# First mixer of a two-block transformer kernel: q and k turned by halves of the tokens, other distances between attention steps, the last v projection moved, one-operation rotation

## The chip, the cores and the metric

The kernel runs on one core of a Trainium2 chip. The metric is the device time of one execution in microseconds (us). Of the kernel before, three runs took 3729.02, 3718.52 and 3720.03 us, a median of 3720.03 us. TensorE (PE) multiplies, PEld is its weight load, VectorE (DVE) and ScalarE (ACT) work element by element, GpSimd (POOL) does small side work, and SyncE (SP) issues the DMAs.

## The reference, cut to what matters

The whole computation is two transformer blocks of two layers each over 512 tokens of width 1024, all in fp32. Only the first layer's mixer is touched, a dilated window attention with 3 groups of 16 heads of 64:

```python
qkv = (h @ w_in).reshape(bsz, seq, 3, 3, 16, 64)
for g, (window, dilation) in enumerate(((128, 1), (512, 4), (2048, 16))):
    q = rope(rms_norm(qkv[:, :, g, 0], q_gain[g]), positions)
    k = rope(rms_norm(qkv[:, :, g, 1], k_gain[g]), positions)
    o, lse = dilated_window_attention(q, k, qkv[:, :, g, 2], window, dilation)
    outs.append(o); lses.append(lse)
alpha = jax.nn.softmax(jnp.stack(lses, axis=0), axis=0)
out = jnp.sum(alpha[..., None] * jnp.stack(outs, axis=0), axis=0)
return out.reshape(bsz, seq, 1024) @ w_out
```

`rope` turns the halves of a head: `[x1*cos - x2*sin, x2*cos + x1*sin]`.

## The kernel before, in words

Every fp32 operand is split into a high and a low fp32r part (`split`: ACT copies the high part, DVE subtracts for the low one), and a product is three matmuls: high by high, low by high, high by low. All matmuls carry line L225. The weights of a step come by DMA (`wraw`), four steps ahead, and are split into `wh` and `wl`.

The mixer (`layer_a_`, L579) works in four quarters `qd` of four heads. In each quarter the groups g = 0, 1, 2 follow each other:

- `wide` (L883) projects q and k together, 512 columns by 128 tokens, for two halves of the tokens; each half gives two PSUM banks `mm`. Per (quarter, group) that is 96 matmuls of 512 columns. `a_heads` (L545) takes each bank into `qs`, makes the norm and the rotation, and leaves `qr`, 128 tokens by 512 (four buffers, so one group). The rotation is four DVE operations on `qs`: times cosine (L561), the two crossed halves times sine (L563, twice), their sum (L565); L567 is the norm.
- `a_turn` (L650) transposes `qr` on TensorE, four 128x128 blocks into the one `sm` bank, and splits the bank into `qkH` and `qkL`; four such steps for q and k of two pairs of heads.
- v comes from `tokmajor` for g = 0, and for g = 1 and 2 together from a second `wide` behind the q, k of g = 1.
- `a_chain` (L666) is the attention of one group. For g = 0, `a_scores` and `a_near`; for the others `a_scores_far` and `a_far`: scores into `sc` banks, a masked minimum on DVE (L714, L735), exp on ACT (L716, L737) into `pm`, transposes of `pm` into the one `pt` bank, a split into `ptH`, `ptL`, and the product with v into the one `o` bank. `a_stats` turns the softmax sums; after g = 2, `a_merge` weighs the three groups: `sw` is turned into the `sm` bank and split into `swH`, `swL`, small matmuls (12 rows in) spread the weights over `sm` and `sc` banks, and DVE multiplies them into `og` and adds up (L857, L860, L861).
- `proj_out` multiplies a quarter's result with `a_w_out`. It stands behind g = 1 of quarter 1 (for quarter 0), and three times at the end: quarter 2, quarter 1 (`late`), quarter 3.

What sets the order: `a_turn`, `a_chain` and others are generators ("chains"). While `wide` and `proj_out` issue matmuls, `mul` adds their length to a clock `now`, and `tick` (L242) lets a chain go on once the distance it yielded (in ns of matmul time) has passed. `until` (L250) is a drain: it advances the chains at once, with no projection between their steps, until a condition holds. Before the next group's `a_heads` can write `qr`, the old turn must be done (`until(old.done)`); before a v tile is taken, older attention must be done. A scheduler then moves instructions locally where it finds an operand late. The projection's matmuls between attention steps are called filler below.

Of the kernel before, what the change touches and what calls it, by code (L numbers as in the profile page):

```python
# [198 lines left out]
class Net:  # L199
# [345 lines left out]
    def a_heads(self, ps, t, C, Sn):  # L545

        nc = self.nc
        p = self.ap
        qs = p.tile([P, S], F32, tag="qs", name=self.nm("qs"), bufs=1)
        nc.scalar.copy(qs, ps)  # L550
        t2 = p.tile([P, S], F32, tag="r2", name=self.nm("r2"), bufs=1)
        nc.scalar.activation(t2, qs, AF.Square)
        ss = self.tile("ss", [P, 8], bufs=3)
        nc.vector.tensor_reduce(out=ss, in_=t2.rearrange("p (h d) -> p h d", d=64), axis=AX.X, op=ALU.add)
        rs = self.tile("rs", [P, 8], bufs=3)
        nc.gpsimd.tensor_scalar(out=rs, in0=ss, scalar1=1.0 / 64, scalar2=EPS, op0=ALU.mult, op1=ALU.add)
# [22 lines left out]
    def layer_a_(self, first, norm):  # L579
        nc, A, p = self.nc, self.A, self.ap  # L580
        cst = {}
        for n, s in (("a_m0", [P, 256]), ("a_me", [64, 2, P]), ("a_m1", [P, P]), ("a_m2", [P, P])):
            cst[n] = p.tile(s, F32, name="c_" + n)
            nc.sync.dma_start(cst[n], A[n])
        sel = p.tile([12, 3, 2, P], F32R, name="selr")
        for g in range(3):
            t = self.scr([12, 2, P])
            nc.sync.dma_start(t, A["a_sel"][:, g])
            nc.scalar.copy(sel[:, g], t)
        self.a_proj = 0  # L590

        hs = first.out, [[StrideTiles(x) for x in hk] for hk in first.out]
        prev = tabs = turn = None
        for qd in range(4):
            st = self.tile("st", [P, NT, 3, 8], bufs=2)
            og, merged = [], []
            vs = []
            for g in range(3):
                old, qr, qkT = turn, [], [[], []]
                for half, ps in self.wide(hs[g > 0], self.a_qk_specs(qd, g), None if qd or g else first.wait):  # L600
                    if tabs is None:
                        first.wait(1)
                        with self.tc.issue_after(self.pow):
                            self.load_cols(COLS[0], "a")
                            tabs = self.rope_tables_a()
                    if old:
                        self.until(lambda: old.done)
                    qr += [self.a_heads(ps[i], 2 * half + i, *tabs[g]) for i in range(2)]
                turn = self.spawn(self.a_turn(qr, qkT, prev))
                if g == 0:  # L610
                    ps = self.tokmajor(hs[0], "a_w_in", 0, 2048 + qd * 256)
                    if prev:
                        self.until(lambda: all(x[2] for x in prev[3]))
# [4 lines left out]
                elif g == 1:  # L618
                    for half, ps in self.wide(hs[1], self.a_v_specs(qd)):
                        if half == 0:  # L620
                            self.until(lambda: prev[2])
                            vs += [self.a_v(), self.a_v()]
                        for i in range(2):
                            for x in range(2):
                                self.split(*(y[:, 2 * half + i] for y in vs[1 + x]), ps[i][:, x * 256:(x + 1) * 256])

                state = [turn, False, False, [prev] if prev else []]
                self.spawn(self.a_chain(qd, g, qkT, vs[g], cst, sel, st, og, merged, state, prev))
                prev = state
                if qd == 1 and g == 1 or qd == 3 and g == 2:  # L630
                    self.until(lambda: len(pend) == 2)
                    self.proj_out("a_w_out", 0, (qd - 1) * 256, pend)
                    self.a_proj = qd
            if qd == 1:
# [12 lines left out]
    def a_v(self):  # L647
        return [self.tile("v" + s, [P, NT, 256], F32R, 2) for s in "HL"]

    def a_turn(self, qr, out, prev):  # L650

        if prev:
            yield lambda: prev[1]
        yield 10000
        for j in range(2):
            for pr in range(2):
                pt = self.small([P, S])
                c = j * 256 + pr * P
                for t in range(NT):
                    self.tr(pt[:, t * P:(t + 1) * P], qr[t][:, c:c + P], P)  # L660
                H, L = self.tile("qkH", [P, S], F32R, 4), self.tile("qkL", [P, S], F32R, 4)
                self.split(H, L, pt)
                out[j].append((H, L))
                yield 1800

    def a_chain(self, qd, g, qkT, vb, cst, sel, st, og, merged, state, prev):  # L666

        yield lambda: state[0].done and (prev is None or prev[2])
        qT, kT = qkT
        ml = self.tile("ml", [P, 5 if g == 0 else 4, 2, 4], bufs=6)  # L670
        ogs = [self.tile("og", [P, S], bufs=6) for _ in range(2)]
        og.append(ogs)
        sc = lambda hd: self.a_scores(g, qT[hd // 2], kT[hd // 2], hd, ml, cst)
        if g == 0:
            todo = [sc(0)]
            yield 2500
            for hd in range(4):
                if hd < 3:
                    todo.append(sc(hd + 1))
                    state[1] = hd == 2  # L680
                yield from self.a_near(todo[hd], vb, hd, ogs)
        else:
            todo = []
            for pr in range(2):
                todo += self.a_scores_far(g, qT[pr], kT[pr], pr, ml, cst)
                state[1] = pr == 1
                yield 2400
            yield from self.a_far(todo, vb, ogs)
        state[2] = True
        yield from self.a_stats(g, ml, st)  # L690
        if g == 2:
# [27 lines left out]
    def a_scores_far(self, g, qT, kT, pr, ml, cst):  # L719

        nc = self.nc
        sc = [self.bank("sc", [P, S]) for _ in range(2)]
        pm = [self.tile("pm", [P, S], bufs=4) for _ in range(2)]
# [32 lines left out]
    def a_near(self, pm, v, hd, ogs):  # L756
# [6 lines left out]
        for b in range(2):  # L763
# [4 lines left out]
            yield 1800  # L768
# [6 lines left out]
    def a_far(self, pms, v, ogs):  # L775

        todo = None
        for n in range(5):
# [17 lines left out]
                    self.nc.scalar.copy(dst.rearrange("p (i n) -> p i n", i=2), o[rows, :, hh])  # L796
            todo = new
            if n < 4:
                yield 1800

    def a_stats(self, g, ml, st):

# [19 lines left out]
    def a_merge(self, qd, og, st, sel, merged):  # L822
# [24 lines left out]
        yield 1800  # L847
        acc = [None, None]
        for g in range(3):
            for pr in range(2):  # L850
# [102 lines left out]
    def a_specs():  # L953
        out = lambda qd: Net.out_specs("a_w_out", 0, qd * 256, 2)
        for qd in range(4):
# [4 lines left out]
            yield from Net.a_v_specs(qd)  # L960
            if qd == 1:
                yield from out(0)
            yield from Net.a_qk_specs(qd, 2)
            if qd == 3:
                yield from out(2)
        yield from out(1)
        yield from out(3)
# [808 lines left out]
```

## Time and profile before

| what | us |
|---|---|
| runs, median (lowest, highest) | 3720.03 (3718.52, 3729.02) |
| the profiled execution | 3730.9 |
| its span | 3729.1 |
| PE busy over the span | 3642.7 |
| first 800 us: PE, DVE, ACT busy | 748.37, 508.37, 376.30 |

The first mixer lies in the first 780 us or so. PEclk is the share of full clock that TensorE was granted: 1.00 is 2.4 GHz and 0.50 is 1.2 GHz; a mean between them says what part of a stretch ran at which. A busy PE at 0.50 does half the work. So a stretch loses time in two ways, and in both the row of a window shows it: the stretch less PE's busy time is idle, and (1 - PEclk) times the busy time went to the low clock.

### The profile page before, as it was taken

The page shows a single profiled execution, that of the slowest core. Times are in us where ns is not written, and L with a number is a line of the kernel's source. Part 1 is how long each engine was busy: PE and PEld are TensorE (multiplying, and loading weights), DVE is VectorE, ACT ScalarE, POOL GpSimd, SP SyncE. Part 2 cuts the span into 40 slices and gives each one's busy share as a digit, 9 for nine tenths or more (in the row PEclk, how much of TensorE's full clock was granted, in tenths as well). Part 3 has the DMA queues.
Part 4 walks back from the last instruction along what each step waited for, and adds up shares of the span by engine and source line. Part 5 has one row for each costly group of instructions (what it writes and reads, how often), then busy time and mean ns, then how long its engine had stood idle before and what let it go on. Part 6 is the DMA issues. An engine that isn't in the chain of part 4 may idle for free.

```text
span 3729.1 us, 48425 instructions
## 1 busy us (share of the span) xinstructions
PE 3642.7 (98%) x19242; PEld 3140.6 (84%) x19242; DVE 2032.5 (55%) x3591; ACT 1382.6 (37%) x2494; POOL 189.2 (5%) x212
## 2 busy tenths in 40 slices
PE   8999999989999999999999999999999999999999
PEld 7888788878889898888888888888898888888887
DVE  6565656677634667333765368743343334784333
ACT  4444444532224643222322246422232223553222
POOL 2111111000000110000000000000000000000000
PEclk9899898999999999999999999999999999999999
DMA  4111111237632224333664322343333332312332
GB/s 131 46 57 57 57 58 45 68 123 245 198 107 67 67 74 166 105 96 108 226 197 163 99 79 62 126 134 97 96 94 99 96 102 76 89 57 87 100 96 74
DMA packets 326843, 384.77 MB, mean 103 GB/s; under 512 B 17354, under 2 KB 299736, under 8 KB 326616
## 3 DMA queue, kind: packets, MB, share of 16 engines
q1 hardware_dynamic: 326616, 381.67, 32.5%
q8 instruction: 151, 2.47, 0.3%
q14 instruction: 76, 0.62, 0.1%
HBM read 379.52 MB, written 2.10 MB: 102 GB/s over the span
## 4 chain that ended last, share of the span: by engine, by line
PE 92%; DVE 3%; ACT 2%; issue 2%; DMA 1%; POOL 0%; SPq 0%; ACTq 0%; POOLq 0%
PE mm L225 54%; PE sc L225 31%; PE sm L225 3%; PE o L225 2%; PE pt L225 2%; DVE wl L317 1%; ACT wh L316 0%; DMA wraw<-in_a_w_in 0%; DVE ptL L317 0%; ACT ptH L316 0%; ACT pm L737 0%; DVE og L860 0%; ACT qkH L316 0%; DVE qr L561 0%; DVE qkL L317 0%
## 5 line engine op out<-in xcount | busy, mean ns | idle before, releaser
L317 DVE TENSOR_TENSOR wl<-wraw,wh 128x1024 fp32r<-128x1024 f32 (+2 forms) x565 | 672.8, 1192 | 841.9 <-ACT wh L316 837.5
L316 ACT CAST wh<-wraw 128x1024 fp32r<-128x1024 f32 (+2 forms) x565 | 577.5, 1024 | 1217.6 <-issue 411.6
L225 PE MATMUL mm<-hL,wh 128*128 128x512 f32 (+2 forms) x1576 | 582.0, 373 | 2.2 <-DVE hL L125 1.8
L225 PE MATMUL mm<-hH,wl 128*128 128x512 f32 (+2 forms) x1576 | 580.8, 372 | 0.0
L225 PE MATMUL mm<-hH,wh 128*128 128x512 f32 (+2 forms) x1576 | 567.7, 373 | 9.7 <-ACT hH L124 5.8
L225 PE MATMUL sc<-hH,wl 128*128 128x512 f32 (+1 forms) x1264 | 461.6, 367 | 0.0
L225 PE MATMUL sc<-hL,wh 128*128 128x512 f32 (+1 forms) x1264 | 461.1, 367 | 0.0
L225 PE MATMUL sc<-hH,wh 128*128 128x512 f32 (+1 forms) x1264 | 452.4, 367 | 0.0
L225 PEld LDWEIGHTS mm<-hL,wh 128*128 128x128 f32 (+1 forms) x1576 | 296.9, 188 | 54.1 <-DVE hL L125 2.2
L225 PEld LDWEIGHTS mm<-hH,wh 128*128 128x128 f32 (+1 forms) x1576 | 287.6, 188 | 63.3 <-ACT hH L124 7.2
L225 PEld LDWEIGHTS mm<-hH,wl 128*128 128x128 f32 (+1 forms) x1576 | 296.9, 188 | 51.8
L225 PE MATMUL mm<-wh,hH 128*128 128x512 f32 (+1 forms) x896 | 328.3, 369 | 3.7 <-ACT hH L316 2.1
L225 PE MATMUL mm<-wl,hH 128*128 128x512 f32 (+1 forms) x896 | 319.7, 360 | 1.5 <-DVE wl L317 1.5
L225 PE MATMUL mm<-wh,hL 128*128 128x512 f32 (+1 forms) x896 | 320.9, 359 | 0.0
L225 PEld LDWEIGHTS sc<-hH,wl 128*128 128x128 f32 x1264 | 240.1, 190 | 38.1
L225 PEld LDWEIGHTS sc<-hL,wh 128*128 128x128 f32 x1264 | 240.4, 190 | 37.8
L225 PEld LDWEIGHTS sc<-hH,wh 128*128 128x128 f32 x1264 | 234.6, 190 | 37.3
L225 PEld LDWEIGHTS mm<-wh,hH 128*128 128x128 f32 x896 | 219.9, 246 | 16.2 <-issue 2.6
L225 PEld LDWEIGHTS mm<-wl,hH 128*128 128x128 f32 x896 | 218.9, 245 | 10.5 <-DVE wl L317 1.7
L225 PEld LDWEIGHTS mm<-wh,hL 128*128 128x128 f32 x896 | 220.7, 246 | 8.1 <-issue 1.5
L225 PE MATMUL mm<-gH,wl 128*128 128x512 f32 x528 | 207.4, 393 | 0.0
L225 PE MATMUL mm<-gH,wh 128*128 128x512 f32 x528 | 206.3, 393 | 0.0
(422 smaller groups left out, 6002.5 us busy)
## 6 DMA issues: line engine op xcount, KB each, us to landing
wraw<-in_ffn_w_gu SPq DMA_DIRECT2D x176, 512.0 KB
ada<-in_w_ada SPq DMA_DIRECT2D x144, 512.0 KB
wraw<-in_ffn_w_down SPq DMA_DIRECT2D x96, 512.0 KB
wraw<-in_ffn_w_gate_up SPq DMA_DIRECT2D x88, 512.0 KB
wraw<-in_a_w_in SPq DMA_DIRECT2D x128, 256.0 KB
wraw<-in_ffn_w_down SPq DMA_DIRECT2D x48, 384.0 KB
wraw<-in_w_in SPq DMA_DIRECT2D x34, 512.0 KB
wraw<-in_b_w_in SPq DMA_DIRECT2D x24, 512.0 KB
```

Source lines behind the costliest of these rows:

```text
L225: self.nc.tensor.matmul(out, lhsT, rhs, **kw)
L316: self.nc.scalar.copy(H, src)
L317: return self.nc.vector.tensor_tensor(out=L, in0=src, in1=H.bitcast(F32), op=ALU.subtract).ins
```

## The change

All edits are in the first mixer.

- Rotation: the two L563 operations of 256 become one of 512 that reads `qs` with the halves of each head exchanged.
- Turn by halves: each half of `wide` spawns its own `a_turn`, with two steps of 512 columns (both pairs of heads, 256 tokens) instead of one turn with four steps; `until` waits for the same half's turn of the group before. `qkH` and `qkL` hold both pairs in one tile, two buffers each.
- Distances: 10000 becomes 12000 before a turn, 1800 becomes 2600 between its steps and between the steps of `a_near`, `a_far` and `a_merge`, 2500 becomes 4000 and 2400 becomes 5000 behind the scores, 1300 becomes 1600 or 4500 between the groups of the merge.
- Late v: in quarter 3 the `wide` of v stands behind the q, k of g = 2. The attention of g = 2 there (`spare`) starts its scores once g = 1's scores are out and v is there, with `pm` in buffers of `hH`.

```diff
-        for a, o in ((0, 32), (32, 0)):
-            nc.vector.tensor_tensor(out=v4(t2)[:, :, :, a:a + 32], in0=v4(qs)[:, :, :, o:o + 32],
-                                    in1=tb(Sn, a, 32), op=ALU.mult)
+        v5 = lambda x: x.rearrange("p (a h u d) -> p a h u d", a=2, h=4, u=2)
+        nc.vector.tensor_tensor(out=v5(t2), in0=v5(qs)[:, :, :, ::-1], op=ALU.mult,
+                                in1=Sn[:, t].rearrange("p a (u d) -> p a u d", u=2)[:, :, None].to_broadcast([P, 2, 4, 2, 32]))
...
-                    if old:
-                        self.until(lambda: old.done)
-                    qr += [self.a_heads(ps[i], 2 * half + i, *tabs[g]) for i in range(2)]
-                turn = self.spawn(self.a_turn(qr, qkT, prev))
+                    if old[half]:
+                        self.until(lambda: old[half].done)
+                    qr = [self.a_heads(ps[i], 2 * half + i, *tabs[g]) for i in range(2)]
+                    turns[half] = self.spawn(self.a_turn(half, qr, qkT, prev))
...
+                if g == 1 and qd < 3:
+                    values(qd, vs, prev)
+                before, prev = prev, state
                 if qd == 1 and g == 1 or qd == 3 and g == 2:
+                    if qd == 3:
+                        values(qd, vs, first_state)
                     self.until(lambda: len(pend) == 2)
...
-        yield 10000
+        yield 12000
         for j in range(2):
+            pt = self.small([P, 2, S // 2])
             for pr in range(2):
-                pt = self.small([P, S])
                 c = j * 256 + pr * P
-                for t in range(NT):
-                    self.tr(pt[:, t * P:(t + 1) * P], qr[t][:, c:c + P], P)
-                H, L = self.tile("qkH", [P, S], F32R, 4), self.tile("qkL", [P, S], F32R, 4)
-                self.split(H, L, pt)
-                out[j].append((H, L))
-                yield 1800
+                for i in range(2):
+                    self.tr(pt[:, pr, i * P:(i + 1) * P], qr[i][:, c:c + P], P)
+            if not out[j]:
+                out[j] += [self.tile("qk" + x, [P, 2, S], F32R, 2) for x in "HL"]
+            H, L = out[j]
+            self.split(H[:, :, HALF[half]], L[:, :, HALF[half]], pt)
+            yield 2600
...
-                todo += self.a_scores_far(g, qT[pr], kT[pr], pr, ml, cst)
+                if spare:
+                    yield lambda: len(vs) == 3
+                todo += self.a_scores_far(g, qT[pr], kT[pr], pr, ml, cst, spare)
                 state[1] = pr == 1
-                yield 2400
+                yield 5000
...
-            yield 1300
+            yield 4500 if g else 1600
```

What that moves on TensorE, at three places. A line of "..." marks rows left out.

First, TensorE in quarter 0, where the last turn of group 2 (`sm<-ident,qr`) meets the scores of the group before (`sc<-qkH`). Before:

```order
L225 MATMUL mm_1835<-wl_1508,hH_185 128x512
L225 MATMUL sm_1786<-ident,qr_1550 128x128
...
L225 MATMUL sm_1786<-ident,qr_1685 128x128
L225 MATMUL sc_1842<-qkH_1791,qkH_1773 128x128
L225 MATMUL sc_1843<-qkH_1791,qkH_1773 128x128
L225 MATMUL sm_1795<-ident,qr_1550 128x128
...
L225 MATMUL sm_1795<-ident,qr_1685 128x128
L225 MATMUL sc_1842<-qkL_1792,qkH_1773 128x128
```

Now:

```order
L225 MATMUL mm_1794<-wl_1492,hH_183 128x512
L225 MATMUL sm_1827<-ident,qr_1661 128x128
...
L225 MATMUL sm_1827<-ident,qr_1675 128x128
L225 MATMUL sc_1850<-qkH_1715,qkH_1648 128x128
...
L225 MATMUL sc_1851<-qkH_1715,qkL_1649 128x128
L225 MATMUL mm_1794<-wh_1491,hH_185 128x512
...
L225 MATMUL mm_1931<-wh_1685,hL_172 128x256
L225 MATMUL sc_1850<-qkH_1715,qkH_1648 128x128
```

Before, the scores follow four transposes whose split they read, and 22 stand together; now the 12 scores behind the transposes read the tokens of the first half, turned earlier, and 14 filler matmuls stand before the first one that reads the new half.

At the first near scores of quarter 0, likewise, 22 filler matmuls now stand between the turn's last transposes and the scores that read them; before, none did.

Second, TensorE at the change from quarter 0 to quarter 1, where the merge (`swH,selr`) of the old quarter meets the turns and the first near scores of the new one. Before:

```order
L225 MATMUL mm_2544<-wl_2165,hH_185 128x512
L225 MATMUL sm_2248<-swH_2194,selr 128x512
L225 MATMUL sm_2248<-swL_2195,selr 128x512
L225 MATMUL sm_2258<-ident,qr_1813 128x128
...
L225 MATMUL sm_2258<-ident,qr_2044 128x128
L225 MATMUL sc_2327<-qkH_2263,qkH_2206 128x256
L225 MATMUL sc_2328<-qkH_2263,qkH_2206 128x256
L225 MATMUL sm_2288<-swH_2194,selr 128x512
```

Now:

```order
L225 MATMUL mm_2806<-wl_2262,hH_185 128x512
L225 MATMUL sc_2427<-swH_2372,selr 128x512
L225 MATMUL sc_2445<-swH_2372,selr 128x512
L225 MATMUL o_2413<-ptH_2461,vH_2098 128x256
L225 MATMUL sm_2423<-swH_2372,selr 128x512
L225 MATMUL sm_2423<-swL_2373,selr 128x512
...
L225 MATMUL pt_2517<-ident,pm_2386 128x128 x3
L225 MATMUL sm_2440<-swH_2372,selr 128x512
L225 MATMUL sm_2440<-swL_2373,selr 128x512
L225 MATMUL sc_2487<-qkH_2229,qkH_2179 128x256
```

The merge now stands among the near attention instead of among the turns. Behind it 157 matmuls without filler follow each other in quarters 1 and 2 each (100 in quarter 3, 132 in quarter 0); before, the longest stretches without filler at those places were 50 and 95 matmuls in each of quarters 1 to 3, and 105 in quarter 0. In quarter 3 the merge's first steps now have 19 filler matmuls ahead of them and 19 more behind them.

Third, TensorE at the end of the mixer, where `mm<-hH` and `mm<-hL` are the late output projection and `mm<-oH` behind `selr` the last one. Before:

```order
L225 MATMUL pt_6916<-ident,pm_6829 128x128
L225 MATMUL pt_6916<-ident,pm_6830 128x128
...
L225 MATMUL o_6925<-ptH_6903,vH_6129 128x256
L225 MATMUL o_6925<-ptL_6904,vH_6129 128x256
...
L225 MATMUL sc_6983<-swH_6975,selr 128x512
```

Now:

```order
L225 MATMUL o_6727<-ptL_6672,vH_6346 128x256
...
L225 MATMUL sm_6854<-ident,s_6848 128x8 x3
L225 MATMUL mm_6796<-hH_6700,wh_6328 128x512
...
L225 MATMUL mm_6830<-hH_6702,wl_6329 128x512
L225 MATMUL o_6764<-ptH_6723,vH_6346 128x256
...
L225 MATMUL sc_6887<-swH_6879,selr 128x512
```

Before, 116 matmuls of attention and merge stand behind the last filler; now 42 do, and the 48 matmuls of the late projection stand among the attention of groups 1 and 2.

## Rows read from the trace of the kernel before

**Rows 1.** The page: busy time of each engine; granted clock in 40 slices.

```profile
PE 3642.7 (98%) x19242; PEld 3140.6 (84%) x19242; DVE 2032.5 (55%) x3591; ACT 1382.6 (37%) x2494; POOL 189.2 (5%) x212
...
PEclk9899898999999999999999999999999999999999
```

**Rows 2.** Windows: stretch, its length, busy us per engine (instructions), PEclk, DMA.

```profile
0.00:800.00 800.00, 748.37 (x3975) 658.84 (x3976) 508.37 (x1174) 376.30 (x927) 119.31 (x124) 0.93 0.21 64
76.00:92.00 16.00, 13.12 (x50) 10.94 (x50) 10.50 (x23) 7.17 (x18) 2.12 (x2) 0.68 0.37 112
116.00:144.00 28.00, 25.73 (x121) 20.86 (x120) 12.04 (x41) 15.02 (x45) 0.00 (x0) 0.63 0.00 1
200.00:208.00 8.00, 6.00 (x53) 5.05 (x52) 6.05 (x9) 3.24 (x5) 0.00 (x0) 1.00 0.57 181
382.00:394.00 12.00, 9.81 (x77) 8.63 (x76) 9.97 (x30) 6.19 (x16) 2.12 (x2) 0.86 0.40 124
557.00:571.00 14.00, 12.00 (x90) 10.77 (x89) 11.94 (x33) 7.54 (x23) 2.67 (x4) 0.76 0.31 100
254.00:274.00 20.00, 16.82 (x71) 13.71 (x70) 16.31 (x39) 9.67 (x29) 0.96 (x2) 0.66 0.22 74
439.00:461.00 22.00, 17.88 (x66) 13.59 (x65) 18.02 (x42) 9.52 (x29) 3.21 (x4) 0.61 0.16 48
614.00:632.00 18.00, 13.88 (x58) 10.94 (x57) 14.22 (x35) 9.16 (x29) 0.00 (x0) 0.62 0.18 58
298.00:312.00 14.00, 12.43 (x97) 9.41 (x94) 6.01 (x12) 7.68 (x18) 0.00 (x0) 1.00 0.01 2
732.00:749.00 17.00, 14.87 (x94) 12.31 (x94) 9.91 (x49) 12.27 (x44) 0.00 (x0) 0.70 0.10 32
749.00:768.00 19.00, 12.37 (x57) 9.50 (x56) 13.84 (x20) 4.78 (x11) 0.00 (x0) 0.64 0.00 0
```

**Rows 3.** Waits of PE, 0 to 800 us: total, times, longest.

```profile
PE sm L225 <- DVE qkL L317: 9.4, 7, 2.3
PE sc L225 <- ACT qkH L316: 8.2, 11, 2.1
PE mm L225 <- ACT oH L316: 5.2, 1, 5.2
...
PE sm L225 <- DVE og L860: 4.6, 4, 1.7
```

**Rows 4.** Timeline of PE, 200 to 206 us: start, length, idle and releaser in brackets.

```profile
201.29 0.39 PE L225 MATMUL mm<-wl,hH 128*128 128x512 f32 x1
201.52 0.60 PE L225 MATMUL sm<-ident,qr 128*128 128x128 f32 x4
203.07 0.33 PE L225 MATMUL sc<-qkH,qkH 64*128 64x128 f32 x2 [0.95 <-ACT qkH L316]
204.45 0.66 PE L225 MATMUL sm<-ident,qr 128*128 128x128 f32 x4 [1.05 <-DVE qkL L317]
```

**Rows 5.** Timeline of PE, 440 to 446 us.

```profile
441.53 0.50 PE L225 MATMUL sm<-swH,selr 12*128 12x512 f32 x1 [2.33 <-DVE qkL L317]
...
443.37 1.11 PE L225 MATMUL sm<-ident,qr 128*128 128x128 f32 x4 [1.11 <-DVE og L860]
```

**Rows 6.** Groups of DVE, 0 to 800 us: count, busy, mean ns, idle before.

```profile
L563 DVE TENSOR_TENSOR r<-qs,a_S 128x256 f32<-128x256 f32 x96 | 36.9, 425 | 2.7 <-POOL a_S L540 1.5
L561 DVE TENSOR_TENSOR qr<-qs,a_C 128x512 f32<-128x512 f32 x48 | 33.6, 700 | 15.5 <-ACT qs L550 13.5 <-PE sm L225 1.8
...
L317 DVE TENSOR_TENSOR ptL<-pt,ptH 128x448 fp32r<-128x448 f32 x32 | 19.8, 619 | 37.8 <-ACT ptH L316 37.8
L714 DVE CUSTOM_DVE_ANT_0 pm<-sc,c_a_m 128x256 f32<-128x256 f32 x48 | 18.3, 418 | 21.4 <-PE pt L225 17.1 <-PE sc L225 4.1
...
L861 DVE TENSOR_TENSOR og<-og,og 128x512 f32<-128x512 f32 x12 | 12.7, 1066 | 0.2
...
L860 DVE TENSOR_TENSOR og<-og,sm 128x512 f32<-128x512 f32 x8 | 8.2, 1029 | 5.8 <-PE sm L225 5.8
```

More of the change, by code (lines that the diff above doesn't have):

```diff
@@ L592, in layer_a_, with values @@
         hs = first.out, [[StrideTiles(x) for x in hk] for hk in first.out]
-        prev = tabs = turn = None
+        prev = tabs = None
+        turns = [None, None]
+        def values(qd, vs, done):
+            for half, ps in self.wide(hs[1], self.a_v_specs(qd)):
+                if half == 0:
+                    self.until(lambda: done[2])
+                    new = [self.a_v(), self.a_v()]
+                for i in range(2):
+                    for x in range(2):
+                        self.split(*(y[:, 2 * half + i] for y in new[x]), ps[i][:, x * 256:(x + 1) * 256])
+            vs += new
         for qd in range(4):
             st = self.tile("st", [P, NT, 3, 8], bufs=2)
-            og, merged = [], []
-            vs = []
+            og, merged, vs = [], [], []
             for g in range(3):
-                old, qr, qkT = turn, [], [[], []]
+                old, turns = turns, [None, None]
+                qkT = [[], []]
                 for half, ps in self.wide(hs[g > 0], self.a_qk_specs(qd, g), None if qd or g else first.wait):
@@ L605, in layer_a_ @@
                             tabs = self.rope_tables_a()
-                    if old:
-                        self.until(lambda: old.done)
-                    qr += [self.a_heads(ps[i], 2 * half + i, *tabs[g]) for i in range(2)]
-                turn = self.spawn(self.a_turn(qr, qkT, prev))
+                    if old[half]:
+                        self.until(lambda: old[half].done)
+                    qr = [self.a_heads(ps[i], 2 * half + i, *tabs[g]) for i in range(2)]
+                    turns[half] = self.spawn(self.a_turn(half, qr, qkT, prev))
+                state = [turns, False, False]
                 if g == 0:
@@ L612, in layer_a_ @@
                     if prev:
-                        self.until(lambda: all(x[2] for x in prev[3]))
+                        self.until(lambda: before[2])
                     vs.append(self.a_v())
@@ L617, in layer_a_ @@
                         self.split(vs[0][0][:, sl], vs[0][1][:, sl], ps[b].rearrange("p (t n) -> p t n", t=2))
[L618 to L629, printed above, removed]
+                self.spawn(self.a_chain(qd, g, qkT, vs, cst, sel, st, og, merged, state, prev))
+                if g == 1 and qd < 3:
+                    values(qd, vs, prev)
+                before, prev = prev, state
                 if qd == 1 and g == 1 or qd == 3 and g == 2:
+                    if qd == 3:
+                        values(qd, vs, first_state)
                     self.until(lambda: len(pend) == 2)
@@ L633, in layer_a_ @@
                     self.a_proj = qd
+                if g == 0:
+                    first_state = state
             if qd == 1:
@@ L648, in a_v, with a_turn, a_chain @@
         return [self.tile("v" + s, [P, NT, 256], F32R, 2) for s in "HL"]
-    def a_turn(self, qr, out, prev):
+    def a_turn(self, half, qr, out, prev):
         if prev:
             yield lambda: prev[1]
-        yield 10000
+        yield 12000
         for j in range(2):
+            pt = self.small([P, 2, S // 2])
             for pr in range(2):
-                pt = self.small([P, S])
                 c = j * 256 + pr * P
-                for t in range(NT):
-                    self.tr(pt[:, t * P:(t + 1) * P], qr[t][:, c:c + P], P)
-                H, L = self.tile("qkH", [P, S], F32R, 4), self.tile("qkL", [P, S], F32R, 4)
-                self.split(H, L, pt)
-                out[j].append((H, L))
-                yield 1800
-    def a_chain(self, qd, g, qkT, vb, cst, sel, st, og, merged, state, prev):
-        yield lambda: state[0].done and (prev is None or prev[2])
-        qT, kT = qkT
+                for i in range(2):
+                    self.tr(pt[:, pr, i * P:(i + 1) * P], qr[i][:, c:c + P], P)
[4 more added lines that the diff above has]
+            yield 2600
+    def a_chain(self, qd, g, qkT, vs, cst, sel, st, og, merged, state, prev):
+        spare = qd == 3 and g == 2
+        yield lambda: all(t and t.done for t in state[0]) and (prev is None or prev[1 if spare else 2])
+        qT, kT = ([[x[:, pr] for x in hl] for pr in range(2)] for hl in qkT)
         ml = self.tile("ml", [P, 5 if g == 0 else 4, 2, 4], bufs=6)
-        ogs = [self.tile("og", [P, S], bufs=6) for _ in range(2)]
-        og.append(ogs)
         sc = lambda hd: self.a_scores(g, qT[hd // 2], kT[hd // 2], hd, ml, cst)
@@ L675, in a_chain @@
             todo = [sc(0)]
-            yield 2500
+            yield 4000
+            ogs = [self.tile("og", [P, S], bufs=6) for _ in range(2)]
             for hd in range(4):
@@ L680, in a_chain @@
                     state[1] = hd == 2
-                yield from self.a_near(todo[hd], vb, hd, ogs)
+                yield from self.a_near(todo[hd], vs[0], hd, ogs)
         else:
@@ L684, in a_chain @@
             for pr in range(2):
-                todo += self.a_scores_far(g, qT[pr], kT[pr], pr, ml, cst)
+                if spare:
+                    yield lambda: len(vs) == 3
+                todo += self.a_scores_far(g, qT[pr], kT[pr], pr, ml, cst, spare)
                 state[1] = pr == 1
-                yield 2400
-            yield from self.a_far(todo, vb, ogs)
+                yield 5000
+            yield lambda: len(vs) == 3 and prev[2]
+            ogs = [self.tile("og", [P, S], bufs=6) for _ in range(2)]
+            yield from self.a_far(todo, vs[g], ogs)
+        og.append(ogs)
         state[2] = True
@@ L717, in a_scores, with a_scores_far @@
         return pm
-    def a_scores_far(self, g, qT, kT, pr, ml, cst):
+    def a_scores_far(self, g, qT, kT, pr, ml, cst, spare):
         nc = self.nc
         sc = [self.bank("sc", [P, S]) for _ in range(2)]
-        pm = [self.tile("pm", [P, S], bufs=4) for _ in range(2)]
+        if spare:
+            pm = [self.hp.tile([P, S], F32, tag="hH", name=self.nm("pm")) for _ in range(2)]
+        else:
+            pm = [self.tile("pm", [P, S], bufs=4) for _ in range(2)]
         for t in range(NT):
@@ L767, in a_near @@
             PT = self.pt_split(pt, 448)
-            yield 1800
+            yield 2600
             for c, n, q0, kt in V[b]:
@@ L798, in a_far @@
             if n < 4:
-                yield 1800
+                yield 2600
     def a_stats(self, g, ml, st):
@@ L846, in a_merge @@
         self.split(H, L, rows)
-        yield 1800
+        yield 2600
         acc = [None, None]
@@ L959, in a_specs @@
             yield from Net.a_qk_specs(qd, 1)
-            yield from Net.a_v_specs(qd)
+            if qd < 3:
+                yield from Net.a_v_specs(qd)
             if qd == 1:
@@ L964, in a_specs @@
             if qd == 3:
+                yield from Net.a_v_specs(qd)
                 yield from out(2)
```

## The prediction

> **What bounds the kernel now.** I read the page first. TensorE is busy for 98% of the span and the others for about half or less, so time can only come from TensorE's idle time and from its clock [rows 1]. The slices of the clock show 8s almost only in the first fifth of the span: the low clock sits in the first mixer, which is all that the change touches. The windows say how much. Over the first 800 us PE idles 51.6 us, and (1 - 0.93) of 748.4 us, about 52 us, go to the clock: some 104 us in all, the most that any order of this mixer could give back. DVE is busy 508 us and ACT 376 us there, so neither bounds the mixer as a whole [rows 2].
>
> The waits name the places [rows 3]. The largest are `sm` waiting for `qkL` and `sc` waiting for `qkH`, 17.6 us together, both a turn that is read too soon; `sm` waiting for `og`, 4.6 us, the merge; and one wait of 5.2 us for `oH` at the very end. From the windows at these places, each loss is idle plus (1 - PEclk) x busy [rows 2]:
>
> - A, first scores of quarter 0, 76 to 92 us: 2.9 + 4.2 = 7.1 us.
> - B, quarter 0's drain, 116 to 144: 2.3 + 9.5 = 11.8.
> - C, last turn meets far scores, at 200, 382 and 557: 2.0 + 3.6 + 4.9 = 10.5.
> - D, merge meets turns at the change of quarter, at 254, 439 and 614: 8.9, 11.1 and 9.4.
> - E, drain behind each D; the row at 298 stands for three: 1.6 each.
> - F, the end: 732 to 749: 2.1 + 4.5 = 6.6; 749 to 768: 6.6 + 4.5 = 11.1.
>
> That is 81 us. The rest is the start and the step into the next layer, where nothing moves.
>
> **The rotation.** It removes 96 operations of 425 ns and adds 48 that the trace does not have. The nearest row is L561, of the same shape, 700 ns: 48 x (850 - 700) = 7 us less of DVE's work [rows 6]. The ends are one old operation's price, 425 ns (20 us less), and the strided L861's, 1066 ns (10 us more). I take 700. DVE's 292 idle us in these 800 hide all three; I count nothing.
>
> **Turn by halves: C.** Before, the four transposes at 201.52 are followed by scores that read their split (0.95 us of wait), and the next turn waits in the same bank for DVE (1.05 us) [rows 4]. Now 12 scores read the half that was turned earlier, and 14 filler matmuls stand before the rest. A filler matmul takes about 0.23 us, from 201.29 to the next start at 201.52 [rows 4]; an attention matmul takes 12.43 / 97 = 0.128 us [rows 2]. So 14 give over 3 us, more than the 2.0 us wait. The splits do the same 512 columns as before, 48 times. C goes: **-10.5 us**, ends 0 (the wait comes back elsewhere) and -10.5.
>
> **A** goes the same way: 22 filler matmuls, 5 us, stand between the last turn and the scores behind it, against 2.9 us of wait: **-7.1 us**, ends 0 and -7.1.
>
> **Longer distances, and where the drains go: B, D, E.** A distance fills waits only while there is filler. What has not passed by the next drain is done there with nothing between, so larger distances also lengthen drains. In quarter 0 the drain grows from 105 to 132 matmuls, with the scores of both pairs among the transposes, so each step has more other work beside it. At E's rate (1.57 us for 97 matmuls) it would cost 2.1 us, at its own old rate 11.8 x 132/105 = 14.8 us. I take the old 11.8: **0**.
>
> In quarters 1 and 2 the stretch of 50 at D and the drain of 95 at E become one of 157. There the merge and the near scores meet on DVE, in the first 48 matmuls: per merge two products at about 0.70 us (L561), four at 1.03 (L860) and four sums at 1.07 (L861), 9.8 us [rows 6]; two `ptL` splits, 1.2; two heads' mask operations, three of 0.42 each besides the small ones, 2.5 or more: 13.5 us of DVE against some 6 us of PE, 48 x 0.128. So PE waits there, up to 7 us. The nearest row is the same conflict in D, 3.2 to 4.1 us idle, with two waits of 2.33 and 1.11 us [rows 2, 5]; I take 5. Then the clock falls as it does in D, at 5.3 to 7.0 us: 11.5 us each, against 10.5 and 12.7 before (D + E). **0 for both**; ends 157 x 0.0162 = 2.5 us (E's rate) and 5 + 20 = 25 us (the whole stretch at the low clock, 157 x 0.128).
>
> In quarter 3, v no longer stands where it did, and the order has 19 filler matmuls on either side of the merge's first steps, 4 us each, so DVE can follow. 100 matmuls remain without filler: 1.6 us by E's rate, up to 9.4 by D's. I take 4 against 11.0: **-7 us**.
>
> **Late v: F.** 96 matmuls of v, 22 us, and the late projection now stand among the attention of groups 1 and 2. The 732 to 749 part goes: **-6.6 us**, ends 0 and -6.6. The 749 to 768 part stays as it is: after `sw` there is still no filler, DVE must do the merge, and `oH` is late by the same 5.2 us [rows 3]. The moved v passes on SP's queue behind eight loads of q and k; DMA's share in these 800 us is 0.21 [rows 2], so its weights, asked for four steps ahead, are not late. `pm` in `hH` waits for the last matmul of v, and its scores stand behind that anyway.
>
> **Sum:** -10.5 - 7.1 - 7.0 - 6.6 = **-31 us**. The profiled execution took 3730.9 us, 10.9 above the median of the runs; the runs differ by up to 10.5 us, so I cannot say that the losses of this execution are all in the median one. I subtract from the middle of the two, 3725.4: **3694 us**.
>
> A sentence that nothing here rests on: the Trainium skill ("TensorE: Matmul & The Clock Gate", Part 1) advises to reckon the clock's ramp at less than 1% of a typical kernel's span. That would be at most 37 us, where the trace has 52 us in the mixer alone, 1.4% [rows 1, 2]; scaled to it, the clock's part of the sum would shrink by a third and the gain be about 26 us.
>
> **The rivals.** From 0.3%, 11 us, on, about the scatter of the runs, a measurement of this kernel tells a change from none.
>
> 1. *The long stretches hold the low clock (slower).* B and the three stretches of quarters 1 to 3 have 546 matmuls without filler. For it: 116 to 144 is such a drain, and ran at 0.63. Against: 298 to 312 is one too, at 1.00. It decides if the clock falls at the start of each and stays until filler comes: 546 x 0.128 = 70 us, with the old idle of B, D and E, 18 us, makes 88 against 46 before: +42, less A, C and F's 24: +18, **3744**. From 24 us of added loss on, the gains are gone.
> 2. *The waits come back.* A, C and quarter 3's 7 us return in the longer drains, and only F is gained: -6.6, **3719**. For it: PE's work is the same, and so are the DVE and ACT chains. Against: the order shows filler at A and C.
> 3. *The clock does not come back.* The low clock follows the kind of matmul (64 rows in the scores, 12 in the merge) and not the waits. Then only idle time is gained: 2.9 + 6.2 + 3 + 2.1 = 14, **3711**. For it: PE is idle for only 2.3 us of 28 in 116 to 144. Against: the same kinds at 298 run at 1.00. By the Trainium skill ("TensorE: Matmul & The Clock Gate", Part 1) the low level is that of an idle engine, and an engine that works between waits would keep the high one: this change would then return idle time alone. The trace shows the low clock behind the waits at all three places of D [rows 2], but no row tells the waits from the kind of matmul.
> 4. *The drains run like E.* With more of other work beside each step, no stretch loses the clock: 546 x 0.0162 = 9 us against 46, -37, with A, C and F -61: **3664**.
>
> **How the numbers follow.** Forecast 0.45, rival 4 0.15, rival 3 0.13, rival 2 0.13, rival 1 0.14. Faster by over 0.3% (below 3709): the forecast but for 0.02, rival 4 and half of rival 3: 0.65. Slower by over 0.3% (above 3731): rival 1's 0.14. The rest, 0.21, is within 0.3%. The range of 8 in 10 goes from 3668, which leaves out the larger half of rival 4, to 3720, which leaves out rival 1: the terms' ends of quarters 1 and 2, some -10 to +13 each, fit in it.
>
> **What would show it.** A and C: no wait of `sc` for `qkH` or `sm` for `qkL` above 1 us except in the merges, their sum well below 17.6 us, and PEclk near 1.00 at the first scores and at the ends of the turns. B and quarters 1 and 2: PEclk near 0.6 over a stretch of 15 to 25 us each, with PE waiting for `og`. Quarter 3: less of that. F: one wait for `oH` of about 5 us remains, with the low clock before it for half as long. Rotation: 48 operations near 0.7 us. The forecast is wrong if the mixer, up to the first matmul of the next layer, is not 20 to 45 us shorter; wrong in mechanism if the gain comes from idle time alone, or from B.

## The result and the profile after

The changed kernel takes 3690.24 us (median of 4 runs, 3686.75 to 3692.58), the kernel before in the same runs 3724.53: a ratio of 0.9908, 95% interval 0.9887 to 0.9929, faster by 34 us. The profiled execution has a span of 3687.9 us, 41.2 less than before. The mixer, up to the first matmul of the next layer (`mm<-hH`), ends at 744.1 us instead of 779.8: 35.7 us of it. The other 5.5 us lie in later layers, which have the same instructions.

The page after: busy time, clock in 40 slices [as rows 1].
```profile
PE 3626.2 (98%) x19242; PEld 3132.9 (85%) x19242; DVE 2026.0 (55%) x3543; ACT 1385.3 (38%) x2494; POOL 213.8 (6%) x212
...
PEclk9998999999999999999999999999999999999999
```
The windows after, columns as in [rows 2]: the whole mixer, the first scores (A), the three places of C, then the drains of quarters 0 to 3, and the end in two parts.
```profile
0.00:745.00 745.00, 717.89 (x3834) 637.00 (x3835) 490.07 (x1095) 373.05 (x910) 143.33 (x123) 0.93 0.22 67
72.00:88.00 16.00, 16.00 (x84) 14.91 (x84) 14.13 (x27) 9.15 (x19) 5.27 (x5) 1.00 0.34 103
184.00:192.00 8.00, 8.00 (x58) 6.60 (x56) 7.18 (x10) 4.37 (x6) 1.29 (x3) 1.00 0.61 195
367.00:375.00 8.00, 8.00 (x51) 6.34 (x49) 7.09 (x9) 4.73 (x7) 1.79 (x3) 1.00 0.62 196
532.00:540.00 8.00, 8.00 (x50) 6.57 (x48) 7.33 (x10) 4.97 (x7) 2.12 (x2) 1.00 0.56 168
108.00:134.00 26.00, 23.73 (x151) 19.32 (x151) 13.44 (x57) 18.00 (x61) 0.00 (x0) 0.87 0.00 1
259.70:298.20 38.50, 37.20 (x159) 28.12 (x158) 21.41 (x48) 15.25 (x41) 0.00 (x0) 0.54 0.00 1
442.90:477.00 34.10, 32.88 (x159) 24.77 (x158) 19.56 (x44) 14.08 (x38) 0.00 (x0) 0.65 0.00 1
622.00:646.00 24.00, 22.08 (x90) 17.25 (x89) 17.04 (x32) 12.39 (x32) 2.77 (x2) 0.64 0.08 23
700.00:718.00 18.00, 15.93 (x88) 12.32 (x86) 12.60 (x27) 7.89 (x16) 0.00 (x0) 1.00 0.30 89
718.00:733.00 15.00, 8.44 (x46) 7.38 (x46) 11.76 (x18) 2.77 (x6) 0.00 (x0) 0.66 0.00 0
```
The same window of before, up to its end of the mixer:
```profile
0.00:781.00 781.00, 730.38 (x3838) 641.04 (x3839) 496.98 (x1144) 370.05 (x911) 118.61 (x123) 0.93 0.21 64
```
Read the two whole-mixer rows against each other: PE's idle time fell from 50.6 to 27.1 us, its busy time from 730.4 to 717.9, and the granted clock is 0.93 in both. Two thirds of the gain are idle time; the low clock hardly became less, it moved. Added up over the stretches at the low level, up to 779.8 and 744.1 us, PE was busy there for 100.6 us before and 94.3 after; at half the speed that difference is worth about 3 us. The other 9 us of the 12 us less busy time are no clock: the same number of matmuls (3830 records each) kept PE busy for a shorter time. One cause can be estimated: a filler matmul is 0.40 us long, but the next starts 0.23 us after it [rows 4], so a matmul in front of a gap counts some 0.17 us more, and the waits of over 0.15 us fell from 55 to 23: 32 x 0.17 = 5 us. No run separates this part. The low clock left A and C (1.00, no idle time at all) and most of quarter 0's drain, and gathered in the long drains of quarters 1 and 2, which run at 0.54 and 0.65.

The waits of PE after, 0 to 800 us [as rows 3]:
```profile
PE mm L225 <- ACT oH L316: 5.4, 1, 5.4
...
PE o L225 <- DVE ptL L317: 3.5, 4, 1.5
...
PE sc L225 <- ACT qkH L316: 0.9, 2, 0.5
...
PE sm L225 <- DVE qkL L317: 0.2, 1, 0.2
```
The 17.6 us of waits for `qkL` and `qkH` are 1.1 now, and the wait for `oH` stands as it was. How the clock falls in quarter 1's drain is seen in PE's timeline (as rows 4; idle time would stand in brackets):
```profile
259.37 0.40 PE L225 MATMUL mm<-wl,hH 128*128 128x512 f32 x1
259.70 0.73 PE L225 MATMUL sc<-swH,selr 12*128 12x512 f32 x2
...
260.67 0.49 PE L225 MATMUL sm<-swH,selr 12*128 12x512 f32 x1
...
262.54 1.11 PE L225 MATMUL pt<-ident,pm 64*128 64x64 f32 x4
263.58 0.79 PE L225 MATMUL sm<-swH,selr 12*128 12x512 f32 x1
...
280.98 0.53 PE L225 MATMUL o<-ptL,vH 128*128 128x192 f32 x1 [1.02 <-DVE ptL L317]
```
The same small matmul takes 0.49 us at 260.67 and 0.79 at 263.58, and no row between has a bracket: the clock fell in a stretch in which PE waited for nothing. The drain's first wait, 1.02 us for DVE, comes 17 us later.

DVE's rotation and the merge's sums [as rows 6]:
```profile
L563 DVE TENSOR_TENSOR r<-qs,a_S 128x512 f32<-128x512 f32 x48 | 33.3, 694 | 3.1 <-POOL a_S L540 1.9
```
```profile
L882 DVE TENSOR_TENSOR og<-og,og 128x512 f32<-128x512 f32 x12 | 12.6, 1058 | 0.1
```

### The profile page after: what moved, and what is told of

It is laid out like the page before. It is cut to its first block, busy times and chain, and to the rows that moved or that the text cites. A ratio compares the mean times of both kernels' runs of the same rounds, so it can differ in the third digit from the quotient of the medians.

```text
span 3687.9 us, 48373 instructions
## 1 busy us (share of the span) xinstructions
PE 3626.2 (98%) x19242; PEld 3132.9 (85%) x19242; DVE 2026.0 (55%) x3543; ACT 1385.3 (38%) x2494; POOL 213.8 (6%) x212
## 4 chain that ended last, share of the span: by engine, by line
PE 94%; DVE 2%; issue 2%; ACT 2%; DMA 0%; POOL 0%; SPq 0%; ACTq 0%; POOLq 0%
PE mm L225 55%; PE sc L225 32%; PE sm L225 3%; PE o L225 2%; PE pt L225 2%; DVE wl L317 0%; DMA og<-in_x 0%; POOL rs L377 0%; DVE og L882 0%; ACT wh L316 0%; DVE ptL L317 0%; ACT pm L758 0%; DVE u L1508 0%; DVE og L881 0%; ACT ptH L316 0%
```

## The experiments

Each kernel was timed in five rounds beside the kernel before; ratios are to it.

**Without the one-operation rotation.** The changed kernel with the two old products (L563 to L565 as before).


> The changed kernel with the old rotation, two crossed DVE products of 256 columns instead of one of 512. Theory (hidden): DVE idles some 290 us in the first 800, so the 96 operations come back at about 425 ns and nobody waits for them: the same as the changed kernel, about 3690 us, within 4 us, and the mixer ends near 744 us. Rival (DVE-bound at the merges and turns): qr comes 0.15 us later per token block, 48 x 0.15 = 7 us, and more where a drain waits for it: 3697 us or more, the mixer's end at 751 us or later.


Measured: 3680.78 us (3678.47 to 3687.00), ratio 0.9887 (0.9870 to 0.9903). The intervals overlap with the changed kernel's. DVE's 96 old operations cost 426 ns each, as expected, and no one waits for them. What differs is the clock: the drains of quarters 1 and 2 take 32.5 and 33.0 us instead of 38.5 and 34.1, at 0.68 and 0.69. With the old distances the sign turns (3691.21 without, 3685.01 with the new rotation, below). So the rotation itself is worth nothing measurable; in both pairs 6 to 10 us go with where the low clock falls.

**Late v undone.**
```diff
-                if g == 1 and qd < 3:
+                if g == 1:
...
-        spare = qd == 3 and g == 2
+        spare = False
```


> The changed kernel with v of quarter 3 back behind the q, k of its group 1, and no early scores of group 2. Theory (late v is worth the tail, term F with part of quarter 3): the tail has 88 matmuls without filler instead of 42, 14 us are lost again behind the start of quarter 3 and none before it: about 3704 us (3697 to 3711). Rival (the tail's gain is from the longer distances and the halves): within 4 us of the changed kernel's 3690.


Measured: 3702.45 us (3701.81 to 3704.41), ratio 0.9944 (0.9931 to 0.9956), which lies clear of the changed kernel's. Late v is worth 12 us beside the new distances. Up to quarter 3 this edit changes nothing, and quarter 1's drain runs at 0.54 here too, so its low clock is not the chance of one execution:
```profile
257.00:296.00 39.00, 37.70 (x159) 28.55 (x159) 21.87 (x52) 15.38 (x42) 0.00 (x0) 0.54 0.00 1
```

**Old distances.**
```diff
-        yield 12000
+        yield 10000
...
-            yield 2600
+            yield 1800
...
-                yield 5000
+                yield 2400
```


> The changed kernel with the old distances (10000, 1800, 2500, 2400, 1300). Theory (the halves give A and C, late v gives F, the distances only move losses into longer drains): about 3690 us, between 3682 and 3698, with A (first scores of quarter 0) and C still without a wait of over 1 us. Rival (the distances do it: they keep a step's operand from being read too soon): A and C's 17.6 us of waits and low clock come back, 3705 to 3712 us.


Measured: 3685.01 us (3677.99 to 3691.38), ratio 0.9898 (0.9881 to 0.9914): no difference. The distances are not what the gain comes from. Its windows show how much the clock decides. These are the drains of quarters 1 and 2, 116 matmuls of the same kinds in each:
```profile
266.90:292.10 25.20, 23.12 (x118) 17.83 (x117) 9.51 (x31) 11.95 (x33) 0.00 (x0) 0.64 0.00 1
447.20:466.00 18.80, 16.34 (x117) 12.14 (x116) 9.11 (x28) 11.31 (x32) 0.00 (x0) 1.00 0.00 1
```
PE idles 2.1 us in the first and 2.5 in the second, the longest waits are 0.68 and 0.37 us in the one and 0.68 and 0.47 in the other, and yet one loses the clock and the other doesn't: 6.4 us. So neither the kinds of matmuls nor the waits of a drain alone decide it.

**Only the distances,** on the kernel before.


> The kernel before with only the new distances; whole turns, v of quarter 3 early, old rotation. Theory (the halves are needed for A and C): the waits of sc for qkH and sm for qkL stay, the stretches without filler grow from 50 + 95 to about 135 to 157 matmuls, and the time stays within 8 us of the kernel before, 3716 to 3732. Rival (the distances do it): 15 to 30 us faster than the kernel before, 3694 to 3709.


Measured: 3738.41 us (3723.43 to 3744.07), ratio 1.0030 (1.0017 to 1.0044): slower by 6 to 16 us, so both expectations missed. The profiled run was its fastest one and doesn't show the loss. It does show C's waits unchanged (about 1 us for `qkH` and 1 us for `qkL` at each of the three places) and drains of 125 to 130 matmuls, three of them with 11 to 24 us at the low clock, where [rows 2] had 1.00 at 298. A did gain: its wait for `qkH` is 1.0 us instead of 2.1, at the full clock. So with whole turns the longer distances help at A, leave C as it was, and lengthen the drains behind D.

**Halves and late v** without the other two, and **halves alone.**


> Halves and late v alone: the changed kernel with the old distances and the old rotation. Theory (the halves and the late v carry the whole gain, distances and rotation only shift where the low clock falls): as fast as the changed kernel or up to 12 us faster, 3676 to 3691. Rival (distances and rotation each help, but only in the other's presence): 3695 us or more.

> Halves alone: old distances, old rotation, v of quarter 3 early. Theory of the prediction (halves give A and C, 17.6 us, and leave D, where the merge meets the turns, as it was): about 3705 us, 3700 to 3710. Rival (halves dissolve D as well, three times 9 to 11 us, because the turn's second half no longer stands between the merge's matmuls): 3685 to 3697 us.


Measured: 3691.21 us (3686.72 to 3693.36), ratio 0.9907 (0.9893 to 0.9922), the changed kernel's own; and 3695.50 us (3684.70 to 3701.57), ratio 0.9913 (0.9895 to 0.9930). Halves alone give some 28 us, well over the 17.6 that the prediction gave them, and so the rival of that run holds: they dissolve D too. Two windows of the halves alone, the time of the merge and the drain behind it:
```profile
254.00:274.00 20.00, 20.00 (x88) 15.67 (x88) 14.29 (x28) 5.07 (x16) 0.00 (x0) 0.91 0.00 1
275.80:301.00 25.20, 23.47 (x127) 18.27 (x126) 10.24 (x31) 12.39 (x34) 0.00 (x0) 0.65 0.00 1
```
D's 3.2 us of idle time and most of its low clock are gone; the clock is lost behind it instead. Beside the old distances late v is worth 4 us, within the scatter.

**The merge on 96 rows,** in the changed kernel and in the kernel before.
```diff
-        sel = p.tile([12, 3, 2, P], F32R, name="selr")
+        sel = p.tile([96, 3, 2, P], F32R, name="selr")
...
-        rows = self.small([12, S])
+        rows = self.small([96, S])
```


> The changed kernel with the merge's small matmuls on 96 rows instead of 12: rows 13 to 96 hold zeros on both sides, the products and the order are the same. Theory (the low clock follows the kind of matmul: in the changed kernel it began at 262.7 and 447.0 us among these matmuls with no wait ahead): the low stretches of 41 and 24 us in quarters 1 and 2 begin later or not at all, 10 to 25 us less, 3665 to 3680. Rival (it follows waits or the lack of filler, whatever the rows): the same low stretches, within 5 us of 3690.

> The kernel before with the merge's small matmuls on 96 rows instead of 12, rows 13 to 96 holding zeros; its waits for qkL and og in the merges (D, up to 2.3 us each) stay. Theory (waits bring the low clock there, as the prediction read D): within 6 us of the kernel before, 3718 to 3730, low clock at all three D. Rival (the 12-row kind does): D's low clock, 5.7 + 7.0 + 5.3 = 18 us, goes: 3703 to 3712.


Measured: the changed kernel so 3679.34 us (3676.56 to 3682.04), ratio 0.9877 (0.9863 to 0.9891); the kernel before so 3717.83 us (3711.20 to 3723.27), ratio 0.9978 (0.9969 to 0.9988). In the kernel before, D stays as it was, waits and low clock, with 96 rows [rows 2 had 0.66, 0.61 and 0.62]:
```profile
243.00:261.00 18.00, 13.88 (x59) 10.98 (x58) 13.48 (x35) 8.55 (x24) 0.00 (x0) 0.65 0.20 63
424.00:446.00 22.00, 17.89 (x68) 13.80 (x68) 17.16 (x41) 9.94 (x29) 2.53 (x2) 0.62 0.18 54
597.00:614.00 17.00, 12.89 (x57) 10.27 (x57) 12.94 (x29) 8.08 (x23) 0.00 (x0) 0.69 0.20 62
```
So the 12 rows are not what brings the low clock there. That the waits do is likely, but scores and transposes stand there as well, and this run does not separate them. The 8 us that this kernel gains lie elsewhere: quarter 0's drain, which ends before the first merge, has its 105 matmuls at 0.94 instead of 0.63 [rows 2]:
```profile
112.00:140.00 28.00, 25.66 (x154) 21.19 (x153) 14.62 (x44) 17.75 (x48) 0.00 (x0) 0.94 0.10 30
```
In the changed kernel the clock falls later with 96 rows, and then behind a wait that was hidden under the low clock before. Its drains of quarters 1 and 2, and TensorE and DVE at that wait:
```profile
258.50:289.60 31.10, 27.78 (x159) 21.76 (x157) 21.11 (x47) 15.31 (x41) 0.00 (x0) 0.77 0.00 1
433.50:465.40 31.90, 29.08 (x159) 22.23 (x157) 19.35 (x44) 14.67 (x39) 0.00 (x0) 0.75 0.00 1
```
```profile
270.83 0.35 PE L225 MATMUL o<-ptH,vH 128*128 128x192 f32 x1
273.38 0.36 PE L225 MATMUL o<-ptL,vH 128*128 128x192 f32 x1 [2.20 <-DVE ptL L317]
```
```profile
268.37 1.04 DVE L884 TENSOR_TENSOR og<-og,sc 128x512 f32<-128x512 f32 x1
269.34 1.03 DVE L885 TENSOR_TENSOR og<-og,og 128x512 f32<-128x512 f32 x1
...
270.99 1.04 DVE L885 TENSOR_TENSOR og<-og,og 128x512 f32<-128x512 f32 x1
...
272.72 0.61 DVE L317 TENSOR_TENSOR ptL<-pt,ptH 128x448 fp32r<-128x448 f32 x1
```
`ptL` stands on DVE behind a product and two sums of the merge. The kind of matmul is not shown to matter: 11 us are hardly more than the 10 us by which the kernel with the old rotation was faster, an edit that nothing waits for.

**The sums left out, or on GpSimd,** both with the merge on 96 rows.
```diff
+                    if qd == 3:
+                        tt(out=i_s(acc[pr]), in0=i_s(acc[pr]), in1=s_i, op=ALU.add)
```


> The changed kernel with the merge on 96 rows, and the merge's sums of the three groups left out in quarters 0 to 2 (four DVE operations of 1.04 us each per merge; the output is then not the reference's). Theory (what is left of the low clock in the drains follows the one wait of 1.9 to 2.6 us of o for ptH or ptL, which stands on DVE behind these products and sums): the waits shrink by half or more and the low stretches of 17, 20 and 14 us at 275, 449 and 620 go or halve: 3660 to 3672 against 3679 with the sums. Rival (the drain's own kind of matmul, 64 rows and short ones, brings the low clock, whatever DVE does): the low stretches stay and the time stays within 4 us of 3679.


```diff
+                    nc.gpsimd.tensor_tensor(out=i_s(acc[pr]), in0=i_s(acc[pr]), in1=s_i, op=ALU.add)
```


> The changed kernel with the merge on 96 rows and the merge's sums on GpSimd instead of DVE; the result is the same. Theory (DVE's merge work makes ptL late, GpSimd idles there): as with the sums left out but for a later last merge, 3662 to 3676. Rival (GpSimd takes so much longer for a sum of 512 columns that the last merge, on the path at the end, and the buffers og wait for it): 3680 or more.


Measured: 3661.86 us (3658.78 to 3664.95), ratio 0.9827 (0.9814 to 0.9840), and 3669.48 us (3664.79 to 3678.53), ratio 0.9850 (0.9834 to 0.9866). With the sums left out (drains of quarters 1 and 2, and the longest waits in the first):
```profile
258.80:283.30 24.50, 22.32 (x159) 17.26 (x157) 16.67 (x42) 15.02 (x41) 0.00 (x0) 1.00 0.00 1
426.80:452.90 26.10, 24.55 (x184) 19.68 (x182) 18.30 (x65) 15.86 (x48) 0.00 (x0) 1.00 0.00 1
```
```profile
271.24 0.63 PE L225 MATMUL sm<-ident,qr 128*128 128x128 f32 x4 [0.70 <-DVE qkL L317]
```
This is the clearest run of the study. The 157 matmuls of quarter 1 take 24.5 us instead of 31.1 (or 38.5 in the changed kernel). Idle time fell by only 1.1 us, 3.3 to 2.2, and busy time by 5.5; before, (1 - 0.77) x 27.78 = 6.4 us had gone to the clock. With DVE's four sums of one merge in its way, PE had one wait of 2.2 us, and the low clock behind it cost about three times that wait. With the sums on GpSimd the same drain still has waits of 1.1 us for `ptH` and 0.8 for `qkL`, and still loses the clock:
```profile
256.80:287.40 30.60, 28.03 (x159) 21.88 (x157) 16.92 (x42) 15.28 (x41) 6.18 (x4) 0.76 0.01 1
```
Quarter 2's drain runs at 1.00 there, as with the sums left out.

**Late v in every quarter.**
```diff
-                if g == 1 and qd < 3:
-                    values(qd, vs, prev)
...
+                if g == 2:
+                    values(qd, vs, first_state)
```


> The changed kernel with v of groups 1 and 2 late in every quarter, so that its 96 matmuls and the output projection stand among the attention; the longest stretches without filler fall from 132, 157, 157, 100 to 39, 39, 119, 64 matmuls. Theory (the low clock needs a long stretch without filler): the mixer's 53 us of low clock fall to 15 to 30, 3655 to 3680. Rival (short stretches lose as much, as at A and C before): 3685 to 3700.


Measured: 3677.98 us (3677.20 to 3681.43), ratio 0.9875 (0.9862 to 0.9889). The whole mixer is at 0.98 instead of 0.93, its idle time 30.2 us:
```profile
0.00:728.00 728.00, 697.85 (x3838) 617.17 (x3839) 488.98 (x1096) 371.75 (x911) 131.18 (x123) 0.98 0.22 69
```
The longest stretches without filler fall, quarter by quarter, from 132, 157, 157 and 100 matmuls to 39, 39, 119 and 64. The clock is 1.00 up to the stretch of 119, falls for part of it (0.89), and is low again only at the end of the mixer (0.84):
```profile
0.00:440.00 440.00, 427.20 (x2337) 381.47 (x2338) 296.72 (x642) 224.72 (x535) 94.91 (x92) 1.00 0.25 79
440.00:470.00 30.00, 28.59 (x173) 23.64 (x171) 21.72 (x69) 17.51 (x52) 6.45 (x6) 0.89 0.01 3
640.00:728.00 88.00, 72.89 (x409) 59.44 (x409) 61.34 (x148) 41.64 (x112) 1.64 (x1) 0.84 0.22 71
```

**All three together:** late v in every quarter, 96 rows, 15 of the 16 sums on GpSimd.


> All three together: v of groups 1 and 2 late in every quarter, the merge's matmuls on 96 rows, its sums on GpSimd but for the very last one, which stays on DVE beside GpSimd's. Alone against the changed kernel's 3690 the first gave 12 us, the second 11, the third 10 on top of the second. Theory (they attack the same low clock in the drains, of which the late v leaves 19 us in the mixer): they overlap, 3662 to 3675, best guess 3668. Rival (they add up): 3655 to 3660. Rival (the late v already took all that the others can give): 3676 to 3680.


Measured: 3653.35 us (3651.13 to 3661.08), ratio 0.9811 (0.9792 to 0.9831), 37 us below the changed kernel: the gains add up, though I expected an overlap. The mixer ends 38 us earlier still, with the clock at 0.98:
```profile
0.00:708.00 708.00, 682.61 (x3841) 613.10 (x3842) 481.52 (x1083) 372.66 (x913) 157.42 (x142) 0.98 0.23 70
```

## Why the prediction was right, and where it was not

The time came out 4 us from the forecast, and every rival's time lay further off. That it came so close is in part luck, since the sum is made of other things than forecast: of its 31 us, 14 were idle time and 17 clock; of the measured 35.7, 23.5 are idle time, about 3 clock, and 9 busy time at the same clock, of which the prediction had no term. By parts, the starts of the first projection of quarters 1, 2 and 3 and of the next layer (before: 177.0, 360.1, 533.6, 779.8; after: 165.1, 347.8, 512.8, 744.1 us) give:

| part | forecast | measured |
|---|---|---|
| to quarter 1: A and B | -7.1 + 0 | -11.9 |
| quarter 1's projections: C's first, D and E | -2.0 + 0 | -0.4 |
| quarter 2's: C's second, D and E | -3.6 + 0 | -8.5 |
| quarter 3 and the end: C's third, quarter 3, F | -4.9 - 7 - 6.6 | -14.9 |
| sum | -31.2 | -35.7 |

- *A and C* held: no idle time and 1.00 at all four places, waits 17.6 to 1.1 us.
- *B* was put at 0 and gained about 5: quarter 0's drain idles 2.3 us as before, but runs at 0.87 instead of 0.63. The runs show that this is the least certain kind of term: the same 105 matmuls ran at 0.63 in the kernel before and at 0.94 in that kernel with 96 rows.
- *Quarters 1 and 2* are the step that failed, though its sum is near. The prediction said that PE waits 5 us for DVE and that the clock falls behind the wait, 11.5 us each. PE idles 1.3 and 1.2 us, and the clock costs (1 - 0.54) x 37.2 = 17 and (1 - 0.65) x 32.9 = 11.5 us: 18 and 13 us. The expected conflict with DVE was there, but the low clock began without a wait and, PE being slow, covered most of it: 1.0 us was left in quarter 1. Where the clock stayed up longer, with 96 rows, it was 2.2 us. PE did not wait for `og` in these two drains at all, which the prediction had named as the sign. That is rival 1's mechanism at two of its four places, with 41 and 24 us at the low level. It did not outweigh the gain: the idle time between the starts of quarters 1, 2 and 3 fell from 7.7 and 9.3 us to 1.3 and 1.2, the clock cost 14 and 2 us more, and busy time at the same clock fell by 8 and 2 us. That last part, without a term in the forecast, is what makes quarter 1's row of the table come out near it.
- *Quarter 3* was mis-sized: 622 to 646 still loses 1.9 + 0.36 x 22.1 = 9.9 us, where 4 were left in the forecast.
- *F* held in its sum: 732 to 749 became 700 to 718 at 1.00, but its 2.1 us of idle time stayed, so that part gave 4.5 us of the 6.6; the wait for `oH` is 5.4 us as forecast, and the low clock at the end costs 2.9 us instead of 4.5, which the forecast had left as it was.
- *Rotation* held: 694 ns instead of the estimated 700, and nobody waits.
- *The mechanism of the gain* was half right. The prediction would have called itself wrong in mechanism for a gain from idle time alone, or from B: it is not idle time alone, but the clock's part, 17 us in the forecast, is about 3, since what A, B and C won in clock went in quarters 1 and 2. In this rival 3 came nearer than the forecast, though not at A and C. Halves were the main part (28 us alone, not 17.6), since they dissolve D as well; the distances, which the prediction credited with moving the drains, give nothing beside them and cost 11 us without them.

On rival 3, whether the low clock follows the kind of matmul or the waits: in the kernel before, the 12 rows are not it (96 rows change nothing at D), and with the waits gone, in the halves alone, that place ran at 0.91. In the long drains it can begin with PE at work 97% of the time, and what starts it there stays open: the kind, the short matmuls, or where the stretch lies. By the rule of the Trainium skill that rival 3 quoted ("TensorE: Matmul & The Clock Gate", Part 1), that the low level is an idle engine's, 259.7 to 298.2 would have run at the full clock; the trace has 0.54 with 1.3 us idle.

## What to carry to other kernels

Break a turn or transpose chain in halves so that something else always stands between the producer and its reader; that was worth more than any distance. Count the longest stretch without large matmuls, since there a wait of 2 us cost three times itself in clock here: put large matmuls into it, and move off the engine that it waits for what nobody needs yet (here the merge's sums, to GpSimd). Differences below some 10 us between versions of this kernel said nothing about the edit until the clock of the long stretches had been compared.

## What the runs showed of the hardware

- The low clock came in stretches in which TensorE was busy: 37.2 of 38.5 us at 0.54 in the changed kernel. Equal drains of one kernel ran at 0.64 and at 1.00 with 2.1 and 2.5 us of idle time.
- GpSimd's sum of 128x512, strided on one side, took 1558 ns in the run with the sums on GpSimd where DVE took 1058 in the changed kernel (1729 ns in the run of all three together). DVE's products took 1077 ns beside it, 1051 in the run with 96 rows and the sums on DVE:
```profile
L885 POOL TENSOR_TENSOR og<-og,og 128x512 f32<-128x512 f32 x12 | 18.4, 1558 | 98.5 <-DVE og L884 69.9 <-ACT ptH L316 28.6
```
